# Preparation of the next token block, ordered behind the feed-forward unit it was handed over with

## The chip, the cores and the metric

The kernel runs on one core of a Trainium2 chip. The number that counts is the device time of one execution, in microseconds (us); of several runs the median is given. The engines are called by the profile's names too: TensorE is PE (its weight loads PEld), VectorE is DVE, ScalarE is ACT, GpSimd is POOL, and SyncE, which here only issues DMA transfers, is SP. Each engine runs its instructions strictly in the order of its own queue.

## The reference

One layer of a hybrid decoder: RG-LRU and sliding-window attention side by side, a memory cross-attention, and a gated ConvFFN. It runs for a prompt of 2048 tokens and for 8 samples of 4 tokens (32 more), with a model width of 1024 and a feed-forward width of 3072. The change touches the last part alone:

```python
n3 = rmsnorm(x, p['g_ffn'])
g, ffn_state = causal_dwconv(n3 @ p['w_ffn_gate'], ffn_prev, p['w_ffn_conv'], p['b_ffn_conv'])
x = x + (jax.nn.gelu(g) * (n3 @ p['w_ffn_up'])) @ p['w_ffn_down']
```

The convolution is three taps wide along the tokens. Everything is computed in float32; a product of two matrices is made of three products of rounded parts (a high part and the residual that is left).

## The kernel before, in words

**Phases.** Phase 1 and phase 2 hold the mixers and the cross-attention. Phase 3 is the ConvFFN, from 1078 us of the profiled span to its end. It works on three blocks of tokens (`SB3`: 696, 692 and 660 + 32 columns; blocks 0, 1 and 2 here), and for each block runs a plan of 24 gate units and 12 down units, in the order gate, gate, down. That group of three is called a pair here. A gate unit (`_P3.gate_up`) forms 128 rows of the gate and of the up projection at once by a scheme of seven products of half the width, in place of eight; a down unit (`_P3.down`) multiplies the gated rows of two gate units with their part of the down weights, in eight groups of columns, each of which VectorE adds to `acc` (L1422).

**The gate unit.** TensorE writes the seven products into four areas of the buffers `pg` (one unit's worth in all, so that the next unit waits until they are read). ScalarE copies the first one (`u`, L1372) and half of the gate (`gb`, L1382); VectorE adds the others (`u`, `up`, `gb`, all by `add`, L1353); POOL sets the two columns ahead of the block (L1366, L1368) and keeps the last two (`fcarry`, L1392). Then the convolution and its activation (`gc`: ScalarE L1396, VectorE twice L1398, ScalarE L1399), the product with `up` (L1400), and its split into `ah` (ScalarE) and `al` (VectorE).

**Weights.** Raw weights come by SP into `wr` (L590). For the seven products VectorE forms sums `ws` (L605), and each is split into `pc`, high part by ScalarE (L79), residual by POOL or VectorE (L83). In block 0 the sums' parts are stored for the later blocks (`kept_s`, L616), which load them.

**The preparation.** The seven products need seven operands made from the normalized tokens. `p3_prep(s)` makes them for one block, in four groups of eight steps. A group loads two pieces of the tokens (`x2d`), VectorE scales each by the gain and the norm (`x`, L768), POOL forms differences and sums (`sub`, L756), and `put` splits each of the seven results into `n3s`: ScalarE copies the high part (L79), POOL subtracts for the residual (L83), SP stores it to DRAM (`opd`, L761). That is 8 `x`, 16 `sub`, 28 copies, 28 residuals and 28 stores a block. Pieces `x` and results `n3s` share four buffers. The stored operands are loaded back in the last gate unit of the block (`p3_ops`).

**Where it is handed over.** `p3_prep` is a generator. While block s runs, the preparation of block s + 1 is advanced by one step after the second and one after the fifth product of gate units 4 to 19:

```python
elif 4 <= i < 20 and e % 3 == 1:
    next(ready, None)
```

The preparation of block 0 runs in phase 2 in the same way.

**What sets the order.** The program's order is not the order of the queues. The framework's scheduler goes through time by a model of its own when the kernel is built, and takes for each engine the first instruction in program order that is ready, so one that stands later in the program but is ready sooner goes ahead. A dependency without a semaphore between two instructions of the same engine (`behind`) fixes their order in the queue and nothing else.

## Time and profile before

| | |
|---|---|
| median of 3 runs | 2738.78 us (2737.75 to 2747.58) |
| profiled execution | 2745.93 us |
| its span | 2744.2 us |
| mean granted clock of TensorE | 0.977 |
| busy: TensorE, VectorE, ScalarE, POOL | 95%, 55%, 40%, 35% |
| stores `opd`: number, size, issue to landing | 56, 346 KB, 3.6 us |

The profile comes from one execution, whose own time stands beside its span; its rows are compared with each other, and the medians with medians. A share of busy time is an average over phases. An instruction's row in a timeline gives in brackets how long its engine idled before it and what ended that. L with a number is the line of the kernel that issued an instruction; L137, L79 and L83 are helpers that record the matmul, the high part and the residual for many callers, so there the tile's name tells them apart.

### The profile page before, as it was taken

The page shows a single profiled execution, that of the slowest core. Times are in us where ns is not written, and L with a number is a line of the kernel's source. Part 1 is how long each engine was busy: PE and PEld are TensorE (multiplying, and loading weights), DVE is VectorE, ACT ScalarE, POOL GpSimd, SP SyncE. Part 2 cuts the span into 40 slices and gives each one's busy share as a digit, 9 for nine tenths or more (in the row PEclk, how much of TensorE's full clock was granted, in tenths as well). Part 3 has the DMA queues.
Part 4 walks back from the last instruction along what each step waited for, and adds up shares of the span by engine and source line. Part 5 has one row for each costly group of instructions (what it writes and reads, how often), then busy time and mean ns, then how long its engine had stood idle before and what let it go on. Part 6 is the DMA issues. An engine that isn't in the chain of part 4 may idle for free.

```text
span 2744.2 us, 40972 instructions
## 1 busy us (share of the span) xinstructions
PE 2611.7 (95%) x15221; PEld 2407.4 (88%) x15221; DVE 1518.5 (55%) x2633; ACT 1085.6 (40%) x2071; POOL 954.5 (35%) x928
## 2 busy tenths in 40 slices
PE   7999999998999998888999999999999989999997
PEld 5778888977998887888999998899999989999997
DVE  6476766585442525767676755454444444444445
ACT  5454745474332434443334343333232323232233
POOL 2422211031402344466333344553232424333333
PEclk8899999998999999999999999999999999999998
DMA  6674545366747788766444487764444765444442
GB/s 234 241 230 168 183 158 173 109 243 245 258 165 245 255 268 306 272 242 209 183 161 177 146 314 252 254 216 162 150 160 158 289 214 164 159 158 167 149 154 83
DMA packets 195671, 553.72 MB, mean 202 GB/s; under 512 B 28628, under 2 KB 49364, under 8 KB 192784
## 3 DMA queue, kind: packets, MB, share of 16 engines
q1 hardware_dynamic: 195472, 551.10, 57.9%
q8 instruction: 120, 1.97, 0.3%
q14 instruction: 79, 0.65, 0.1%
HBM read 409.22 MB, written 141.80 MB: 201 GB/s over the span
## 4 chain that ended last, share of the span: by engine, by line
PE 69%; DVE 11%; DMA 6%; issue 4%; ACT 4%; POOL 4%; SPq 1%; POOLq 0%; DVEq 0%; ACTq 0%
PE pg L137 23%; PE pd L137 17%; PE pin L137 10%; PE po L137 5%; PE pmo L137 3%; PE pq L137 3%; DVE gc L1398 3%; POOL pc L83 2%; PE sc L137 1%; DMA x<-x2d 1%; ACT gc L1396 1%; DMA opd<-n3s 1%; POOL x L756 1%; POOL n3s L83 1%; PE tp L853 1%
## 5 line engine op out<-in xcount | busy, mean ns | idle before, releaser
L137 PE MATMUL pg<-n,pc 128*128 128x346 f32 (+1 forms) x6048 | 1022.0, 327 | 48.2 <-DVE up L1353 16.1
L137 PEld LDWEIGHTS pg<-n,pc 128*128 128x128 f32 x6048 | 965.6, 189 | 92.6 <-DVE up L1353 28.2
L83 POOL TENSOR_TENSOR pc<-wr,pc 128x512 fp32r<-128x512 f32 x312 | 411.0, 1322 | 451.4 <-ACT pc L79 446.2
L137 PE MATMUL pd<-ah,pc 128*128 128x346 f32 (+1 forms) x2240 | 467.7, 325 | 18.7 <-DVE acc L1422 12.9
L137 PEld LDWEIGHTS pd<-ah,pc 128*128 128x128 f32 x2240 | 379.4, 191 | 24.7 <-DVE acc L1422 17.6
L79 ACT ACTIVATE pc<-wr 128x512 fp32r<-128x512 f32 x312 | 195.3, 629 | 503.3 <-PE pd L137 236.7
L1422 DVE TENSOR_TENSOR acc<-pd,acc 128x692 f32<-128x692 f32 (+1 forms) x280 | 245.0, 878 | 175.6 <-PE pd L137 172.7
L137 PE MATMUL pd<-al,pc 128*128 128x346 f32 (+1 forms) x1120 | 271.6, 324 | 0.0
L137 PEld LDWEIGHTS pd<-al,pc 128*128 128x128 f32 x1120 | 196.6, 191 | 0.0
L1398 DVE SCALAR_TENSOR_TENSOR gc<-gb,pp,gc 128x696 f32<-128x696 f32 (+2 forms) x144 | 150.1, 1043 | 82.8 <-ACT gc L1396 79.0
L137 PE MATMUL pin<-n1h,wh 128*128 128x512 f32 (+1 forms) x560 | 188.9, 363 | 5.6 <-DVE ql L83 1.8
L137 PE MATMUL pin<-n1h,wl 128*128 128x512 f32 (+1 forms) x560 | 185.8, 358 | 2.8 <-POOL wl L83 2.8
L137 PE MATMUL pin<-n1l,wh 128*128 128x512 f32 (+1 forms) x560 | 186.6, 359 | 1.5 <-DVE n1l L83 1.5
L83 POOL TENSOR_TENSOR wl<-wr,wh 128x1024 fp32r<-128x1024 f32 x35 | 84.7, 2426 | 218.7 <-ACT wh L79 190.8
L1353 DVE TENSOR_TENSOR u<-pg,u 128x346 f32<-128x346 f32 (+1 forms) x144 | 74.3, 516 | 141.0 <-PE pg L137 140.5
L83 POOL TENSOR_TENSOR pc<-ws,pc 128x512 fp32r<-128x512 f32 x72 | 94.5, 1312 | 158.7 <-ACT pc L79 140.6
L1353 DVE TENSOR_TENSOR up<-pg,u 128x346 f32<-128x346 f32 (+1 forms) x144 | 74.1, 515 | 123.5 <-PE pg L137 123.5
L79 ACT ACTIVATE pc<-ws 128x512 fp32r<-128x512 f32 x144 | 90.0, 627 | 113.1 <-PE pg L137 70.0
L137 PEld LDWEIGHTS pin<-n1h,wh 128*128 128x128 f32 x560 | 103.1, 193 | 23.5 <-DVE ql L83 2.4
L1353 DVE TENSOR_TENSOR gb<-pg,u 128x314 f32<-128x314 f32 (+2 forms) x96 | 38.9, 426 | 145.5 <-PE pg L137 145.5
L137 PEld LDWEIGHTS pin<-n1h,wl 128*128 128x128 f32 x560 | 102.6, 193 | 18.8 <-POOL wl L83 3.8
L137 PEld LDWEIGHTS pin<-n1l,wh 128*128 128x128 f32 x560 | 102.7, 194 | 17.1 <-DVE n1l L83 2.6
(317 smaller groups left out, 4196.0 us busy)
## 6 DMA issues: line engine op xcount, KB each, us to landing
pc<-kept_s SPq DMA_DIRECT2D x192, 512.0 KB, 4.3
kept_s<-pc SPq DMA_DIRECT2D x96, 512.0 KB, 3.0
wh<-keeph SPq DMA_DIRECT2D x90, 512.0 KB, 4.0
wl<-keepl SPq DMA_DIRECT2D x90, 512.0 KB, 5.0
wr<-in_w_gate_dram SPq DMA_DIRECT2D x72, 512.0 KB, 3.8
wr<-in_w_down_dram SPq DMA_DIRECT2D x72, 512.0 KB, 4.0
opd<-n3s SPq DMA_DIRECT2D x56, 346.0 KB, 3.6
n<-opd SPq DMA_DIRECT2D x14, 1384.0 KB, 11.2
```

Source lines behind the costliest of these rows:

```text
L79: nc.scalar.activation(hi, src, AF.Copy)
L83: return e.tensor_tensor(out=lo, in0=src, in1=hi.bitcast(F), op=OP.subtract).ins
L137: nc.tensor.matmul(o, w[a], xs, start=first and n == 0, stop=last and n == 2, skip_group_check=more)
L756: sub = lambda o, x, y, op=OP.subtract: nc.gpsimd.tensor_tensor(out=o, in0=x, in1=y, op=op)
L853: nc.tensor.transpose(tp[:, j], st[:, j, c * 128:(c + 1) * 128], K.ident)
L1353: add = lambda o, p, t: nc.vector.tensor_tensor(out=o, in0=p, in1=t, op=OP.add)
L1396: nc.scalar.activation(gc, gb[:, 2:2 + NW], AF.Identity, scale=K.col(C_FW, 48 + f), bias=K.col(C_FB, f))
L1398: nc.vector.scalar_tensor_tensor(gc, gb[:, k:k + NW], K.col(C_FW, 24 * k + f), gc, op0=OP.mult, op1=OP.add)
L1422: nc.vector.tensor_tensor(out=v, in0=pd[:, :, 0:H], in1=v, op=OP.add)
```

## The change

Each of the preparation's operations on VectorE, ScalarE and POOL is given an order dependency on the latest marked operation of its own engine in the gate unit that is being written when the step is handed over. The marks are, on VectorE, each addition `add`; on ScalarE, the copies `u` and `gb`; on POOL, the two columns ahead of the block and the carry. `put` has its two operations written out in place of the helper `split`, so that each can be given its dependency. Loads and stores get none. In phase 2 no marks are set, so the preparation of block 0 gets none either. In the changed kernel the lines of phase 3 stand some lines lower: the scaling is L774, the copies `n3s` are L765, the residuals L766, the stores L767, `add` L1362, `gc` L1408, `acc` L1432.

```diff
--- before.py
+++ after.py
@@ -508,6 +508,7 @@
             self.nc.sync.dma_start(self.x1s, self.I["x"][:, :, SEQ:T].rearrange("k p t -> p k t"))
             smp = _MemSample(self)
             self.xpool = lambda: dict(pool=self.wraw, tag="wr")
+            self.mark = {}
             ready = self.p3_prep(0)
 
             def prep(n=1):
@@ -753,11 +754,16 @@
             a = self.xpool()
             return a.pop("pool").tile(shape, dtype, name=name, **a)
 
-        sub = lambda o, x, y, op=OP.subtract: nc.gpsimd.tensor_tensor(out=o, in0=x, in1=y, op=op)
+        def after(eng, ins):
+            self.behind(ins, self.mark.get(eng), "preparation order")
+
+        def sub(o, x, y, op=OP.subtract):
+            after("pool", nc.gpsimd.tensor_tensor(out=o, in0=x, in1=y, op=op))
 
         def put(nm, k, src):
             t = tile_([128, 2, H], R, "n3s")
-            self.split(src, t[:, 0], t[:, 1], "act", "pool")
+            after("act", nc.scalar.activation(t[:, 0], src, AF.Copy))
+            after("pool", nc.gpsimd.tensor_tensor(out=t[:, 1], in0=src, in1=t[:, 0].bitcast(F), op=OP.subtract))
             nc.sync.dma_start(self.opd[s][BUDDY.index(nm)][:, 2 * k:2 * k + 2], t.bitcast(F))
 
         for k in range(KT // 2):
@@ -765,7 +771,7 @@
             for kk in (k, k + KT // 2):
                 x = tile_([128, W], F, "x3")
                 self.p3_dma(x, [d[kk] for d in self.x2d], t0, W)
-                nc.vector.scalar_tensor_tensor(x, x, self.col(G_FFN, kk), rt, op0=OP.mult, op1=OP.mult)
+                after("dve", nc.vector.scalar_tensor_tensor(x, x, self.col(G_FFN, kk), rt, op0=OP.mult, op1=OP.mult))
                 xs += [x[:, 0:H], x[:, H:W]]
             b11, b12, b21, b22 = xs
             yield
@@ -1350,7 +1356,11 @@
         xy = K.psum([128, 2, 512], "pg", "pg")
         zw = K.psum([128, 2, 512], "pg", "pg")
         X, Y, Z, V = (t[:, e, 0:H] for t in (xy, zw) for e in range(2))
-        add = lambda o, p, t: nc.vector.tensor_tensor(out=o, in0=p, in1=t, op=OP.add)
+        mark = K.mark
+
+        def add(o, p, t):
+            mark["dve"] = nc.vector.tensor_tensor(out=o, in0=p, in1=t, op=OP.add).ins
+
         tmp = lambda nm: q2.tile([128, H], F, name=nm, tag="hv", bufs=3)
 
         def product(i, out, first):
@@ -1363,13 +1373,13 @@
 
         gb = q2.tile([128, NW + 2], F, name="gb")
         if s == 0:
-            nc.gpsimd.memset(gb[:, 0:2], 0.0)
+            mark["pool"] = nc.gpsimd.memset(gb[:, 0:2], 0.0).ins
         else:
-            nc.gpsimd.tensor_copy(gb[:, 0:2], K.p3c[s - 1][:, f])
+            mark["pool"] = nc.gpsimd.tensor_copy(gb[:, 0:2], K.p3c[s - 1][:, f]).ins
         up = q1.tile([128, W], F, name="up")
         product(0, X, True)
         u = tmp("u")
-        nc.scalar.activation(u, X, AF.Copy)
+        mark["act"] = nc.scalar.activation(u, X, AF.Copy).ins
         product(1, Y, True)
         u2 = tmp("u2")
         add(u2, Y, u)
@@ -1379,7 +1389,7 @@
         product(3, V, True)
         add(up[:, H:W], V, u4)
         product(4, X, False)
-        nc.scalar.activation(gb[:, 2:2 + H], X, AF.Copy)
+        mark["act"] = nc.scalar.activation(gb[:, 2:2 + H], X, AF.Copy).ins
         product(5, Z, False)
         n = w - H
         add(gb[:, 2 + H:2 + w], Z[:, 0:n], u2[:, 0:n])
@@ -1389,7 +1399,7 @@
             bt = lambda t: t[:, n:H].rearrange("p (b t) -> p b t", t=NT)
             add(gv[:, :, 2:6], bt(Z), bt(u2))
             nc.gpsimd.tensor_copy(K.sfo[:, f], gv[:, :, 4:6])
-        nc.gpsimd.tensor_copy(self.carry[:, f], gb[:, w:w + 2])
+        mark["pool"] = nc.gpsimd.tensor_copy(self.carry[:, f], gb[:, w:w + 2]).ins
         product(6, V, False)
         add(up[:, 0:H], V, u2)
         gc = q1.tile([128, NW], F, name="gc")
```

The order of the queues, as built, at three places in block 0. The names with numbers are buffers: `x_12431` and `x_12435` are the two pieces of the second group, `t_12497` is its difference, `opd_1` and so on are the stored operands.

ScalarE, around the copies of the second group, in the kernel before:

```order
L79 ACTIVATE n3s<-x_12431 128x346
L79 ACTIVATE pc<-wr 128x512
L79 ACTIVATE pc<-ws 128x512
L79 ACTIVATE n3s<-x_12431 128x346
L1372 ACTIVATE u<-pg 128x348
L79 ACTIVATE pc<-wr 128x512
L79 ACTIVATE n3s<-t_12497 128x346
L79 ACTIVATE pc<-wr 128x512
L79 ACTIVATE pc<-ws 128x512 x2
L79 ACTIVATE n3s<-x_12431 128x346
L1382 ACTIVATE gb<-pg 128x348
```

and in the changed one:

```order
L1382 ACTIVATE u<-pg 128x348
L765 ACTIVATE n3s<-x_12431 128x346
L79 ACTIVATE pc<-wr 128x512
L765 ACTIVATE n3s<-t_12497 128x346
L79 ACTIVATE pc<-wr 128x512
L79 ACTIVATE pc<-ws 128x512 x2
L1392 ACTIVATE gb<-pg 128x348
L79 ACTIVATE pc<-ws 128x512
L79 ACTIVATE pc<-wr 128x512
```

Before, four copies `n3s` stand among eleven rows, two of them ahead of `u`; after, two stand behind `u`, and none in the rest of that unit.

VectorE, where the second group is scaled, before:

```order
L1422 TENSOR_TENSOR acc<-pd,acc 128x696
L605 TENSOR_TENSOR ws<-wr 128x512
L768 SCALAR_TENSOR_TENSOR x_12431<-x_12431,pp,rt 128x692
L1422 TENSOR_TENSOR acc<-pd,acc 128x696
L605 TENSOR_TENSOR ws<-ws,wr 128x512
L1422 TENSOR_TENSOR acc<-pd,acc 128x696
L768 SCALAR_TENSOR_TENSOR x_12435<-x_12435,pp,rt 128x692
L1422 TENSOR_TENSOR acc<-pd,acc 128x696
```

and after:

```order
L1408 SCALAR_TENSOR_TENSOR gc<-gb,pp,gc 128x696 x2
L1362 TENSOR_TENSOR up<-pg,u_12275 128x348
L83 TENSOR_TENSOR pc<-ws,pc 128x512
L1410 TENSOR_TENSOR up<-up,gc 128x696
L774 SCALAR_TENSOR_TENSOR x_12431<-x_12431,pp,rt 128x692
L774 SCALAR_TENSOR_TENSOR x_12435<-x_12435,pp,rt 128x692
L83 TENSOR_TENSOR al<-up,ah 128x696
L1362 TENSOR_TENSOR u_12439<-pg,u 128x348
L1362 TENSOR_TENSOR u_12456<-pg,u_12439 128x348
```

The two scalings stood between the additions `acc` of a down unit; now they stand side by side in a gate unit, behind its product `up<-up,gc` and ahead of `al`.

SP, its stores `opd` and loads around the second group's stores before:

```order
L590 DMA wr<-in_w_gate_dram 128x1024
L761 DMA opd_6_11526<-n3s 128x692
L616 DMA kept_s_3_12417<-pc 128x1024
L590 DMA wr<-in_w_up_dram 128x1024
L731 DMA x_14233<-x2d_68 128x328
L731 DMA x_14233<-x2d_69 128x364
L731 DMA x_14237<-x2d_68 128x328
L731 DMA x_14237<-x2d_69 128x364
L590 DMA wr<-in_w_gate_dram 128x1024
L590 DMA wr<-in_w_up_dram 128x1024
```

and after:

```order
L617 DMA kept_s_0_12776<-pc 128x1024
L767 DMA opd_2_11522<-n3s 128x692
L617 DMA kept_s_1_12798<-pc 128x1024
L617 DMA kept_s_2_12819<-pc 128x1024
L591 DMA wr<-in_w_gate_dram 128x1024
L617 DMA kept_s_3_12871<-pc 128x1024
L767 DMA opd_3_11523<-n3s 128x692
L591 DMA wr<-in_w_up_dram 128x1024
L767 DMA opd_4_11524<-n3s 128x692
```

Before, the second group's last store (`opd_6`) is followed by the loads of the fourth group's pieces (`x_14233`, `x_14237`) within a few rows; after, one or two stores of the second group stand between the raw weights' loads, and no pieces are loaded there.

## Rows read from the trace of the kernel before

**Rows 1.** The page of the whole span: busy time, share of the span and instructions of each engine, and the shares of the chain that ended last.

```profile
PE 2611.7 (95%) x15221; PEld 2407.4 (88%) x15221; DVE 1518.5 (55%) x2633; ACT 1085.6 (40%) x2071; POOL 954.5 (35%) x928
...
PE 69%; DVE 11%; DMA 6%; issue 4%; ACT 4%; POOL 4%; SPq 1%; POOLq 0%; DVEq 0%; ACTq 0%
```

**Rows 2.** Busy time by stretch in block 0 of the feed-forward phase. The first three stretches are one pair each (two gate units and a down unit), the last is the five pairs behind them. Columns: start and end, us; length, us; then for PE, PEld, DVE, ACT and POOL busy us (instructions); granted clock of PE; DMA share; GB/s.

```profile
1150.23:1202.50 52.27, 46.52 (x270) 44.07 (x269) 40.14 (x49) 21.82 (x38) 32.92 (x31) 0.97 0.64 232
1202.50:1256.06 53.56, 45.17 (x272) 42.60 (x271) 38.50 (x43) 21.83 (x39) 34.85 (x33) 1.00 0.64 224
1256.06:1310.74 54.68, 46.46 (x261) 44.13 (x261) 36.18 (x42) 21.05 (x38) 33.94 (x32) 0.94 0.64 220
1310.74:1531.94 221.20, 218.37 (x1323) 209.63 (x1322) 147.79 (x200) 88.39 (x140) 81.64 (x81) 1.00 0.46 167
```

**Rows 3.** The same view and columns in block 1: three pairs, and two pairs in one stretch.

```profile
1715.79:1765.09 49.30, 44.80 (x265) 43.49 (x265) 22.74 (x28) 17.43 (x31) 28.65 (x31) 0.97 0.77 255
1765.09:1811.61 46.52, 43.70 (x266) 41.91 (x265) 24.63 (x30) 17.16 (x32) 30.13 (x32) 1.00 0.72 242
1811.61:1855.64 44.03, 43.04 (x266) 42.01 (x265) 19.62 (x26) 14.05 (x24) 16.97 (x18) 1.00 0.55 188
1855.64:1942.50 86.86, 86.17 (x531) 84.12 (x530) 39.08 (x52) 25.55 (x40) 27.08 (x29) 1.00 0.49 158
```

**Rows 4.** What TensorE waited for in the three pairs of block 0 (1150.23 to 1310.74 us). Columns: engine, operation and line, what it waited for: us in total, times, longest us.

```profile
PE pd L137 <- DVE acc L1422: 7.0, 5, 2.5
PE pg L137 <- DVE gb L1353: 5.8, 5, 1.8
PE pg L137 <- DVE up L1353: 3.6, 4, 2.4
PE pg L137 <- ACT u L1372: 3.3, 1, 3.3
PE pg L137 <- DVE u L1353: 2.5, 2, 1.5
```

**Rows 5.** The first line of the same view for block 1's three pairs (1715.79 to 1855.64 us).

```profile
PE pd L137 <- DVE acc L1422: 5.6, 3, 3.5
```

**Rows 6.** Groups by line on ScalarE in the three pairs of block 0, shapes apart: the copies `n3s`. Columns: line, engine, operation, out<-in with shapes, count | busy us, mean ns of one | idle us just before them and what ended it.

```profile
L79 ACT ACTIVATE n3s<-x 128x346 fp32r<-128x346 f32 x24 | 11.8, 490 | 30.8 <-POOL x L756 12.3 <-DMA opd<-n3s 10.8 <-DVE x L768 7.7
...
L79 ACT ACTIVATE n3s<-t 128x346 fp32r<-128x346 f32 x4 | 1.9, 483 | 0.0
```

**Rows 7.** The same view on POOL: the preparation's residuals, subtractions and additions.

```profile
L83 POOL TENSOR_TENSOR n3s<-x,n3s 128x346 fp32r<-128x346 f32 x24 | 26.4, 1108 | 9.5 <-ACT n3s L79 9.5
...
L756 POOL TENSOR_TENSOR x<-x,x 128x346 f32<-128x346 f32 x8 | 8.5, 1068 | 6.8 <-DVE x L768 4.9 <-issue 1.5
L83 POOL TENSOR_TENSOR n3s<-t,n3s 128x346 fp32r<-128x346 f32 x4 | 5.2, 1300 | 0.0
L756 POOL TENSOR_TENSOR t<-x 128x346 f32<-128x346 f32 x4 | 4.3, 1067 | 5.8 <-DVE x L768 5.8
L756 POOL TENSOR_TENSOR x<-x 128x346 f32<-128x346 f32 x4 | 4.0, 1010 | 0.3
```

**Rows 8.** The same view on VectorE: an operation of the gate, `gc`, and the preparation's scaling `x`.

```profile
L1398 DVE SCALAR_TENSOR_TENSOR gc<-gb,pp,gc 128x696 f32<-128x696 f32 x12 | 15.2, 1265 | 7.4 <-ACT gc L1396 7.3
...
L768 DVE SCALAR_TENSOR_TENSOR x<-x,pp,rt 128x692 f32<-128x692 f32 x8 | 8.4, 1056 | 0.6 <-DMA x<-x2d 0.6
```

**Rows 9.** Timeline around TensorE's stop before 1207.84 us, block 0, rows of four engines in order of time. Columns: start us, length us, engine, line, operation, out<-in, count [idle before <-what ended it].

```profile
1202.30 0.94 DVE L768 SCALAR_TENSOR_TENSOR x<-x,pp,rt 128x692 f32<-128x692 f32 x1 [0.61 <-DMA x<-x2d]
...
1204.36 1.36 POOL L756 TENSOR_TENSOR x<-x,x 128x346 f32<-128x346 f32 x1
...
1206.95 0.49 ACT L79 ACTIVATE n3s<-x 128x346 fp32r<-128x346 f32 x1 [3.62 <-POOL x L756]
...
1207.84 4.47 PE L137 MATMUL pg<-n,pc 128*128 128x348 f32 x26 [3.27 <-ACT u L1372]
```

**Rows 10.** Timeline around TensorE's stop before 1751.97 us, block 1, same columns: ScalarE, VectorE twice, TensorE.

```profile
1745.42 0.49 ACT L79 ACTIVATE n3s<-x 128x346 fp32r<-128x346 f32 x1 [3.55 <-POOL x L756]
...
1747.71 1.91 DVE L1398 SCALAR_TENSOR_TENSOR gc<-gb,pp,gc 128x692 f32<-128x692 f32 x1 [4.51 <-ACT gc L1396]
...
1751.06 0.87 DVE L1422 TENSOR_TENSOR acc<-pd,acc 128x692 f32<-128x692 f32 x1
...
1751.97 0.82 PE L137 MATMUL pd<-ah,pc 128*128 128x346 f32 x2 [3.53 <-DVE acc L1422]
```

**Rows 11.** Groups by line on VectorE in three pairs of block 0 without preparation (1354.88 to 1487.70 us): `gc`.

```profile
L1398 DVE SCALAR_TENSOR_TENSOR gc<-gb,pp,gc 128x696 f32<-128x696 f32 x12 | 12.6, 1051 | 6.8 <-ACT gc L1396 6.6
```

**Rows 12.** Timeline of VectorE in one of those pairs: the product's low part `al`, a weight sum `ws`, and the gate's end with the first `acc` of the down unit.

```profile
1417.04 1.12 DVE L83 TENSOR_TENSOR al<-up,ah 128x696 fp32r<-128x696 f32 x1 [0.85 <-ACT ah L79]
...
1420.63 1.06 DVE L605 TENSOR_TENSOR ws<-wr 128x512 f32<-128x512 f32 x1 [1.01 <-DMA wr<-in_w_up_dram]
...
1426.75 2.15 DVE L1398 SCALAR_TENSOR_TENSOR gc<-gb,pp,gc 128x696 f32<-128x696 f32 x2 [1.10 <-ACT gc L1396]
...
1430.64 1.67 DVE L1422 TENSOR_TENSOR acc<-pd,acc 128x696 f32<-128x696 f32 x2
```

**Rows 13.** What SP's queue waited for in the three pairs of block 0: the line of the stores `opd`. Columns as in rows 4.

```profile
SPq L761 <- POOL n3s L83: 21.6, 12, 4.3
```

**Rows 14.** The same line for block 1's three pairs.

```profile
SPq L761 <- POOL n3s L83: 35.9, 16, 5.8
```

## The prediction

> **What bounds the kernel now.** I read the busy shares of the whole page first [rows 1]. TensorE is busy for 95% of the span, and the chain that ended last runs through it for 69%; VectorE follows with 11%. So time can only be won where TensorE stands still or runs slow, and the question is what it waits for in the stretch that the change touches.
>
> That stretch is the feed-forward phase, and there I read busy time pair by pair, a pair being two gate units and the down unit that follows. In block 0, three pairs in a row take 52.27, 53.56 and 54.68 us and the next five take 221.20 us together, 44.24 each [rows 2]. The work of TensorE is the same in all eight. What differs is the other engines: POOL is busy 33 to 35 us in each of the three and 16.3 in each of the five, VectorE 36 to 40 against 29.6, ScalarE 21 to 22 against 17.7. Block 1 shows the same twice, in smaller: 49.30, 46.52 and 44.03 us, then 86.86 for two pairs, 43.43 each [rows 3].
>
> The groups by line say whose work it is. All eight of VectorE's scalings `x`, all 28 copies `n3s` of ScalarE and all 44 preparation operations of POOL for block 1 lie in those three pairs [rows 6 to 8]. The program hands this work over in units 4 to 19, which is eight pairs, and the queue packs it into the first three.
>
> The excess is my budget. Block 0: 160.51 - 3 x 44.24 = 27.8 us. Block 1: 139.85 - 3 x 43.43 = 9.6 us. Together **37.4 us**. It divides by TensorE's own columns. In block 0 its busy time is 138.15 against 3 x 43.67 = 131.0, so 7.1 us are longer matmuls, where the granted clock is 0.97 and 0.94, and 20.7 us are standing still. The list of its waits agrees: 22.2 us in the three pairs, 7.0 of them for `acc`, 11.9 for VectorE's additions `gb`, `up` and `u`, and 3.3 in one piece for ScalarE's `u` [rows 4]. In block 1 the largest entry is again `acc`, 5.6 us in three waits [rows 5].
>
> How such a wait comes about is plain in two chains. At 1207.84 TensorE had stood for 3.27 us for `u` on ScalarE; `u` had been ready to run, but a copy `n3s` stood ahead of it in ScalarE's queue and waited 3.62 us for POOL's `x`, and that for VectorE's scaling at 1202.30, which itself waited 0.61 us for its load [rows 9]. In block 1 an `n3s` held ScalarE for 3.55 us until 1745.42; the activation `gc` of the gate came behind it, VectorE's `gc` sat idle 4.51 us for that, `acc` came behind `gc`, and TensorE stood 3.53 us for `acc` [rows 10]. Head-of-line blocking by preparation work, in an order that the build chose.
>
> **The change part by part.** It adds no operation and removes none: 8 scalings, 28 copies, 28 residuals, 16 subtractions and additions and 28 stores per block remain. The added dependencies are order on one engine, so they cost no instruction. What moves: each preparation operation now stands behind the gate unit in which it is handed over. The listed order shows one or two copies `n3s` per unit on ScalarE, close behind `u`, where they stood between almost all operations; the two scalings of a group stand side by side on VectorE between the product `up<-up,gc` and `al`, once in two pairs; and the queue of SP carries a store `opd` or two per unit in place of bursts.
>
> What goes: the three dense pairs of block 0 and the two to three of block 1. If the spread pairs cost nothing, all 37.4 us go. That is the bound on one side.
>
> What is late next, in block 0. Each of its eight pairs now gets an eighth of the work. ScalarE: 28 x 490 ns / 8 = 1.7 us on 17.7 of 44.2; it has room, and a copy behind `u` finds its source finished a unit earlier, as the scaling stands in the unit before. POOL: 44 operations of 1.0 to 1.3 us [rows 7], 48.4 us / 8 = 6.1 us on 16.3; room too. VectorE: one scaling of 0.94 us per pair, as it ran at 1202.30 [rows 9], on 29.6. What is not hidden by itself is the slower VectorE beside a busy POOL. `gc` took 1265 ns in the dense pairs and 1051 in the others [rows 8, 11]. Over all: VectorE's busy time in the three pairs is 114.8 us; less 3 x 29.6 and 8 x 0.94 for the scalings, 18.6 us are stretch, for 44 POOL operations. If that much recurs, it is 2.3 us per pair. Not all of it delays TensorE. In a pair without preparation, the run from `gc` at 1426.75 to the end of `acc` at 1432.3 is the one on which TensorE's restart hangs [rows 12]: 5.6 of VectorE's 29.6 us, so 0.19 x 2.3 = 0.44 us per pair. The two scalings take 1.88 us ahead of `al`, before which VectorE idles 0.85 us [rows 12]: 1.0 us late, in every second pair, 0.5 per pair if all of it arrives. So between 0 and 0.94 us by this working; I take 0.75, nearer the upper end, because the stretches that wait for weights are tight too: 8 x 0.75 = **6 us**. The hard bounds are 0 and the whole stretch of 18.6 us; the bound beyond (that spreading saves nothing) is a rival.
>
> Block 1: its VectorE is busy 19.5 us of 43.4, and its stretch in the three pairs was 66.99 - 3 x 19.54 - 6 x 0.94 = 2.7 us; six scalings, as the three pairs have 84 VectorE instructions and three quiet ones 78 [rows 3]. Its third pair gives a second measure: POOL worked 16.97 - 13.54 = 3.4 us on preparation there and the pair lost 0.6 us [rows 3]; in proportion, 6.1 us per pair would lose 1.1, and eight pairs 8.6. I take **3 us** of bounds 0 and 8.6, nearer the stretch, as that pair also ends what the dense ones left behind.
>
> The stores. A store `opd` waits in SP's queue for POOL's residual, 21.6 us in 12 waits with a longest of 4.3 in block 0, and 35.9 in 16 with a longest of 5.8 in block 1 [rows 13, 14]. In the new order a store stands ahead of a weight load in each pair. I cost this at nothing: the residual is the next of POOL's operations behind a finished copy, and the loads are issued some units ahead; if the cover is gone, the price is the slower rival's. The copies' own wait for a free buffer (10.8 us of their idle time ended with a store's landing [rows 6]) goes, as the four buffers `x` now turn over twice per unit and not as fast as the queue allows.
>
> Sum: 37.4 - 6 - 3 = 28.4 us. The profiled execution took 2745.93 us (span 2744.2, and 1.7 outside it): 2745.9 - 28.4 = 2717.5. The median of the runs is 2738.78, 7.15 below that execution, and by the same gain **2710 us**. A part of the budget is slow clock, 7.1 us in block 0 and 2.3 in block 1 (131.54 us busy against 3 x 43.09); how much of that the median run had is not shown, and the range allows for its absence.
>
> **One rule weighed.** The rows show VectorE's instructions longer while POOL works (`gc` 1265 against 1051 ns [rows 8, 11]). The Trainium skill, "SBUF — State Buffer", section "Who interferes with whom", says that a VectorE instruction with two SBUF inputs contends with a GpSimd instruction that reads SBUF, that whoever issues first keeps the shared pair for its whole instruction, and that the other blocks. By that, the sum of the stretch would depend on how many operations meet and not on how dense they are; `gc` reads two such inputs, and here the trace agrees. By the rule the sum would keep the whole stretch, which is rival (a); by the rows of the edge it keeps a third.
>
> **The rivals.**
> (a) The stretch is kept whole. POOL's 44 operations meet VectorE's as often when spread, and every delay reaches TensorE: 18.6 + 2.7 us stay, the gain is 37.4 - 21.3 = 16 us, 2723. For it: VectorE is the engine that most of the waits name [rows 4]. Against it: VectorE idles 14.7 us of each quiet pair, and not all of its work is awaited.
> (b) The price is per step, not per density. Each of 64 steps costs 37.4 / 64 = 0.58 us wherever it stands, and nothing changes: 2739. For it: each chain of rows 9 and 10 starts with one ordinary step. Against it: block 1's third pair, with 3.4 us of POOL's preparation, lost 0.6 us, and its first, with 15.1, lost 5.9 [rows 3]: 0.18 and 0.39 us for each.
> (c) All is hidden: 2738.8 - 37.4 = 2701. For it: every engine but TensorE has room in each pair. Against it: block 0's VectorE, idle 14.7 us a pair, has less room than block 1's, idle 23.9, and even there the third pair lost something.
> (d) **Slower**, by SP's queue. A store that waits for POOL now stands ahead of a weight load in each of 16 pairs. VectorE in a quiet pair already waits 1.0 us for a weight load [rows 12], so a load held up is passed on. If each pair loses the longest wait of block 0, 4.3 us, it is 69 us against 37.4 won: 2770. It decides from 37.4 / 16 = 2.3 us a pair; the means of the waits are 21.6 / 12 = 1.8 and 35.9 / 16 = 2.2 [rows 13, 14]. Against it: those waits arose while four buffers were turned over as fast as possible.
> That the change does not do what it says is excluded by the order itself.
>
> **How the numbers follow.** The forecast, 2710 with an own range of 2702 to 2719: 0.55. (c) 0.12, (a) 0.13, (b) 0.12, (d) 0.08. A difference of 0.5%, 13.7 us, is about what a measurement of this kernel can tell from no change, so faster means under 2725.1: forecast, (a) and (c), 0.80. Same: (b), 0.12. Slower: (d), 0.08. For 8 in 10 the range takes in the forecast, (a) and (c) with some room: 2698 to 2728.
>
> **What would show it.** In the profile after, all eight pairs of block 0 with preparation take about 45 us and those of block 1 about 43.6; POOL's busy time is about 22 us in each, and not 33 and 16. ScalarE's idle time ahead of `n3s` for POOL's `x` is gone, and so is TensorE's wait of 3.3 us for `u`. TensorE's waits for `acc` shrink to a few tenths each. `gc` lies between 1051 and 1265 ns. If the pairs stand at 46 us and more, (a) or (b) holds: with `gc` still near 1265 ns it is the stretch, otherwise the steps. If SP's waits for `n3s` are long and VectorE's `ws` waits for `wr` by 2 us and more, it is (d). The prediction is wrong if the eight pairs of block 0 do not come out alike.

## The result, and the profile after

The changed kernel takes 2725.4 us (median of 6 runs, 2716.98 to 2729.83) where the kernel before, run beside it, takes 2744.6 (2737.75 to 2747.58): a ratio of 0.9925, with a 95% interval of 0.9906 to 0.9945 (the quotient of the two medians is 0.9930). It is faster by 19.2 us, or 0.7%. The forecast was 28.4 us of gain and 2710; the time lies inside the range of 2698 to 2728, near its upper end, and outside the forecast's own range of 2702 to 2719.

The profiled execution took 2723.25 us, its span 2721.5. Against the 2744.2 of before that is 22.7 us less, but not all of it lies where the change does. The first gate product starts at 1078.2 us in the profile of before and at 1068.9 here, though up to there every queue has the same order in both kernels. From that start to the end of the span, **1666.0 us became 1652.6, 13.4 less**: 11.7 in block 0 (571.4 to 559.8), 0.9 in block 1 (539.4 to 538.5), 0.9 in block 2. The control e8 below settles what the other 9.3 us are.

The busy shares and the chain, the two lines that answer to [rows 1]:

```profile
PE 2601.2 (96%) x15221; PEld 2399.2 (88%) x15221; DVE 1532.7 (56%) x2633; ACT 1084.4 (40%) x2071; POOL 969.6 (36%) x928
...
PE 72%; DVE 11%; ACT 5%; issue 5%; DMA 4%; POOL 2%; SPq 1%; POOLq 0%; DVEq 0%; ACTq 0%
```

TensorE works 10 us less, at a mean granted clock of 0.981 in place of 0.977, and holds 72% of the chain in place of 69%. VectorE, which has the same instructions as before, is busy 14 us longer.

Busy time by stretch, five of the pairs of block 0 with their preparation, which answer to [rows 2] (columns as there):

```profile
1141.08:1190.52 49.44, 45.63 (x273) 43.17 (x273) 38.82 (x47) 18.97 (x31) 25.37 (x21) 1.00 0.51 188
1190.52:1235.11 44.59, 43.33 (x265) 41.55 (x263) 32.96 (x40) 19.17 (x32) 22.59 (x21) 1.00 0.54 198
1235.11:1283.08 47.97, 45.58 (x268) 43.86 (x267) 32.74 (x42) 18.95 (x31) 24.32 (x22) 0.96 0.54 191
...
1327.68:1374.50 46.82, 44.10 (x267) 42.26 (x267) 34.68 (x42) 18.94 (x31) 25.09 (x22) 1.00 0.55 196
1374.50:1419.10 44.60, 43.30 (x265) 41.55 (x264) 32.94 (x40) 19.17 (x32) 22.60 (x21) 1.00 0.53 197
```

The dense pairs of 52 to 55 us are gone, and POOL is busy 22 to 25 us everywhere. But the pairs are not alike: 49.4, 44.6, 48.0, 44.6, 46.8, 44.6, 46.8, 45.2. Every second one is long, and the third has a granted clock of 0.96 besides. Block 1 shows the same in smaller, against [rows 3]:

```profile
1696.81:1741.41 44.60, 43.16 (x265) 41.94 (x265) 22.58 (x28) 13.16 (x21) 18.51 (x18) 1.00 0.48 162
1741.41:1785.32 43.91, 43.26 (x267) 42.05 (x265) 19.96 (x26) 14.20 (x24) 18.40 (x19) 1.00 0.56 189
1785.32:1829.91 44.59, 43.15 (x265) 41.95 (x265) 22.72 (x28) 13.91 (x23) 20.12 (x20) 1.00 0.59 194
```

The long pairs have 28 instructions of VectorE in block 1 and 42 in block 0 (47 in the first), the others 26 and 40: the two scalings of a group. What TensorE waits for in the eight pairs of block 0, which answers to [rows 4]:

```profile
PE pg L137 <- DVE u L1362: 7.4, 10, 2.0
PE pd L137 <- DVE acc L1432: 4.3, 6, 1.2
PE pg L137 <- DVE up L1362: 4.2, 10, 1.0
```

The 3.3 us for ScalarE's `u` do not occur any more, and `acc` fell from 7.0 us in three pairs to 4.3 in eight. At the top stands a wait for VectorE's sums `u`, 7.4 us. In block 1 the entry `acc` of [rows 5] is gone altogether, and `u` leads there too:

```profile
PE pg L137 <- DVE u L1362: 7.4, 10, 1.6
PE pg L137 <- DVE up L1362: 3.1, 9, 0.3
```

ScalarE's copies `n3s`, which had 30.8 us of idle time ahead of them in [rows 6], have 0.3 (groups by line, same columns):

```profile
L765 ACT ACTIVATE n3s<-x 128x346 fp32r<-128x346 f32 x22 | 10.7, 486 | 0.3
...
L765 ACT ACTIVATE n3s<-t 128x346 fp32r<-128x346 f32 x4 | 1.9, 481 | 0.0
```

So the blocking at the head of ScalarE's queue, the mechanism of [rows 9, 10], is removed completely. What replaces it is on VectorE. Its groups in the same eight pairs, against [rows 8, 11]:

```profile
L1408 DVE SCALAR_TENSOR_TENSOR gc<-gb,pp,gc 128x696 f32<-128x696 f32 x32 | 37.8, 1181 | 18.2 <-ACT gc L1406 17.6
...
L83 DVE TENSOR_TENSOR al<-up,ah 128x696 fp32r<-128x696 f32 x16 | 19.8, 1237 | 3.8 <-ACT ah L79 3.8
...
L774 DVE SCALAR_TENSOR_TENSOR x<-x,pp,rt 128x692 f32<-128x692 f32 x8 | 10.6, 1361 | 1.4 <-DMA x<-x2d 1.4
```

`gc` takes 1181 ns (1265 dense, 1051 alone), and a scaling takes 1361 ns in the mean, more than the 1056 of the dense order. That mean hides two lengths: the first scaling of each long pair takes 0.93 us, the second 1.97 to 1.98 in three of them and 1.23 in the third, where it waited 1.4 us for its load. One long pair of block 0 shows the path, VectorE first and then TensorE (timeline, columns as in rows 9):

```profile
1344.44 2.83 DVE L774 SCALAR_TENSOR_TENSOR x<-x,pp,rt 128x692 f32<-128x692 f32 x2
1347.19 1.48 DVE L83 TENSOR_TENSOR al<-up,ah 128x696 fp32r<-128x696 f32 x1
1348.58 1.13 DVE L1362 TENSOR_TENSOR u<-pg,u 128x348 f32<-128x348 f32 x2
...
1356.90 3.32 DVE L1408 SCALAR_TENSOR_TENSOR gc<-gb,pp,gc 128x696 f32<-128x696 f32 x2 [1.10 <-ACT gc L1406]
...
1361.96 1.66 DVE L1432 TENSOR_TENSOR acc<-pd,acc 128x696 f32<-128x696 f32 x2
```

```profile
1349.14 6.09 PE L137 MATMUL pg<-n,pc 128*128 128x348 f32 x36 [1.15 <-DVE u L1362]
...
1362.89 0.59 PE L137 MATMUL pd<-ah,pc 128*128 128x348 f32 x2 [1.16 <-DVE acc L1432]
```

The two scalings take 2.83 us, `al` behind them 1.48, and only then come the sums `u`; TensorE has stood 1.15 us for the first of them when it goes on at 1349.14. Later in the same pair the two `gc` take 3.32 us in place of 2.15 [rows 12], `acc` is late, and TensorE stands another 1.16.

The four long pairs share the first of these two stops and not the second. The longest wait for `u` is 1.16, 1.98, 1.15 and 1.11 us in the first, third, fifth and seventh pair. A stop of 1.1 us for `acc` stands in the fifth and the seventh alone; the first has one of 1.01 for `up` instead. In the third pair, 0.6 us behind the stop of 1.98, the granted clock was at the lower of its two levels, 1.2 GHz, for 3.4 us, and TensorE is busy 45.58 us in that pair where the fifth has 44.10. The stretch at the lower level (columns as in rows 2):

```profile
1258.02:1261.43 3.41, 3.41 (x14) 3.40 (x13) 2.50 (x2) 0.00 (x0) 3.41 (x3) 0.50 0.07 27
```

SP's stores `opd` wait for POOL's residual as in [rows 13, 14], in the eight pairs of block 0 and in block 1:

```profile
SPq L767 <- POOL n3s L766: 24.1, 22, 2.5
```

```profile
SPq L767 <- POOL n3s L766: 63.5, 26, 6.2
```

### The profile page after: what moved, and what is told of

Same layout as the page of the kernel before. It is cut to its first block, busy times and chain, and to the rows that moved or that the text cites. A ratio compares the mean times of both kernels' runs of the same rounds, so it can differ in the third digit from the quotient of the medians.

```text
span 2721.5 us, 41002 instructions
## 1 busy us (share of the span) xinstructions
PE 2601.2 (96%) x15221; PEld 2399.2 (88%) x15221; DVE 1532.7 (56%) x2633; ACT 1084.4 (40%) x2071; POOL 969.6 (36%) x928
## 3 DMA queue, kind: packets, MB, share of 16 engines
q8 instruction: 120, 1.97, 0.3%
## 4 chain that ended last, share of the span: by engine, by line
PE 72%; DVE 11%; ACT 5%; issue 5%; DMA 4%; POOL 2%; SPq 1%; POOLq 0%; DVEq 0%; ACTq 0%
PE pg L137 24%; PE pd L137 19%; PE pin L137 10%; PE po L137 6%; PE pmo L137 3%; DVE gc L1408 3%; PE pq L137 3%; PE sc L137 1%; ACT gc L1406 1%; POOL pc L83 1%; DVE al L83 1%; DMA x<-x2d 1%; PE tp L859 1%; ACT pc L79 1%; DMA x<-in_x_dram 1%
## 5 line engine op out<-in xcount | busy, mean ns | idle before, releaser
L83 POOL TENSOR_TENSOR pc<-wr,pc 128x512 fp32r<-128x512 f32 x312 | 419.2, 1352 | 425.7 <-ACT pc L79 424.8
L1432 DVE TENSOR_TENSOR acc<-pd,acc 128x692 f32<-128x692 f32 (+1 forms) x280 | 244.9, 877 | 178.2 <-PE pd L137 176.5
L1408 DVE SCALAR_TENSOR_TENSOR gc<-gb,pp,gc 128x696 f32<-128x696 f32 (+2 forms) x144 | 150.6, 1046 | 78.5 <-ACT gc L1406 76.1
L1362 DVE TENSOR_TENSOR u<-pg,u 128x346 f32<-128x346 f32 (+1 forms) x144 | 74.2, 515 | 130.7 <-PE pg L137 128.9
L1362 DVE TENSOR_TENSOR up<-pg,u 128x346 f32<-128x346 f32 (+1 forms) x144 | 74.1, 514 | 124.0 <-PE pg L137 124.0
L1362 DVE TENSOR_TENSOR gb<-pg,u 128x314 f32<-128x314 f32 (+2 forms) x96 | 38.8, 425 | 150.9 <-PE pg L137 150.9
```

Source lines behind the costliest of these rows:

```text
L83: return e.tensor_tensor(out=lo, in0=src, in1=hi.bitcast(F), op=OP.subtract).ins
L1362: mark["dve"] = nc.vector.tensor_tensor(out=o, in0=p, in1=t, op=OP.add).ins
L1408: nc.vector.scalar_tensor_tensor(gc, gb[:, k:k + NW], K.col(C_FW, 24 * k + f), gc, op0=OP.mult, op1=OP.add)
L1432: nc.vector.tensor_tensor(out=v, in0=pd[:, :, 0:H], in1=v, op=OP.add)
```

## The experiments

Four lengths from each profile are compared, besides the time: *nine pairs* of block 0, from the end of the first pair's predecessor (1150.23 in the profile of before, 1141.08 after) over the eight pairs with preparation and one more; *ten pairs* of block 1, from the end of block 0's last down unit; the *last nine* of these; and *phase 3*, from the first gate product to the end of the span. All times are in us. A ratio is that to the kernel before, with its interval.

| kernel | nine pairs | ten pairs | last nine | phase 3 | time, ratio |
|---|---|---|---|---|---|
| before | 425.7 | 466.4 | 400.2 | 1666.0 | |
| e8, before again | 428.7 | 467.3 | 401.1 | 1670.0 | 2741.04 (one run) |
| changed | 413.9 | 465.5 | 397.4 | 1652.6 | 2725.4, 0.9925 (0.9906 to 0.9945) |
| e1, no preparation | 399.1 | 457.9 | 390.5 | 1628.9 | 2706.84, 0.9857 (0.9838 to 0.9875) |
| e2, no scalings | 412.2 | 459.6 | 393.8 | 1646.7 | 2720.95, 0.9906 (0.9889 to 0.9922) |
| e3, half a unit later | 414.4 | 461.9 | 396.0 | 1649.7 | 2728.21, 0.9930 (0.9914 to 0.9946) |
| e4, ScalarE alone | 415.3 | 464.5 | 397.4 | 1652.0 | 2726.4, 0.9925 (0.9910 to 0.9941) |
| e5, no POOL | 409.1 | 461.4 | 394.3 | 1643.6 | 2722.64, 0.9914 (0.9896 to 0.9932) |
| e6, no stores | 416.5 | 464.8 | 397.8 | 1653.5 | 2732.38, 0.9947 (0.9927 to 0.9968) |
| e7, residuals on VectorE | 413.9 | 459.5 | 393.7 | 1648.9 | 2722.21, 0.9915 (0.9899 to 0.9932) |
| e9, scalings apart | 409.9 | 463.3 | 396.2 | 1646.5 | 2722.69, 0.9921 (0.9903 to 0.9939) |
| e10, one unit later | 405.5 | 462.0 | 394.9 | 1642.4 | 2719.3, 0.9905 (0.9879 to 0.9931) |
| e11, down units only | 415.0 | 459.0 | 391.9 | 1645.9 | 2724.18, 0.9928 (0.9909 to 0.9946) |
| e12, e10 and residuals | 406.7 | 459.0 | 392.1 | 1639.2 | 2714.72, 0.9896 (0.9878 to 0.9914) |

Each length comes from one profile. The kernel before, which has two, differs by 3.0, 0.9, 0.9 and 4.0 us between them, so two rows that differ by less tell little by their lengths alone. The first of the ten pairs is not to be read for the preparation at all: in the changed kernel it holds none, and its length goes by the clock, 65.8 to 66.2 us in the profiles where its granted clock is 1.00, 66.9 to 67.4 at 0.97, and 68.1 at 0.95, which is the changed kernel's. Its row there and in e2 (columns as in rows 2):

```profile
1628.67:1696.81 68.14, 63.27 (x375) 60.79 (x374) 34.66 (x47) 22.00 (x35) 23.15 (x22) 0.95 0.76 249
```

```profile
1635.60:1701.46 65.86, 60.95 (x375) 58.15 (x374) 35.12 (x47) 22.00 (x35) 24.00 (x23) 1.00 0.78 257
```

**e8, the control.** The kernel before, unchanged.

> The kernel before, unchanged, profiled once more. The feed-forward phase started at 1078.2 us in its first profile and at 1068.9 in the changed kernel's, though all queues stand in the same order up to there. If that difference is the spread of single executions, this one starts anywhere from 1068 to 1079, and from there to the end of the span takes 1666 us within 2. If it belongs to the kernel before, it starts at 1077 to 1079 again.

Phase 3 started at 1069.3 us and took 1670.0. So the start is a spread of single executions: over the fourteen profiles of this study it lies between 1068.9 and 1079.6, without relation to what was edited. The 9.3 us are not the change's, and what the change does in phase 3 is 13.4 or 17.4 us by the one or the other profile of before. The length of 1670 is 4 over the 1666 that was expected to come back within 2. Most of that lies in the second of the dense pairs, which took 52.3, 56.0 and 55.4 this time. TensorE's stops in the second come to 8.4 us in the first profile and to 8.2 in this one; what differs is its granted clock, 0.94 in place of 1.00 (against the second of rows 2):

```profile
1194.98:1251.01 56.03, 47.76 (x271) 45.20 (x270) 39.44 (x43) 21.81 (x39) 33.66 (x33) 0.94 0.60 214
```

The medians' difference of 19.2 us, with an interval of some 15 to 26, holds 17.4 and not 13.4; why the stretch ahead of phase 3 varies was not tried.

**e1, the budget.** The preparation of blocks 1 and 2 is left out:

```diff
-                        ready = self.p3_prep(s + 1) if s < 2 else iter(())
+                        ready = iter(())
+                        if s < 2:
+                            self.opd[s + 1] = [t[:, :, 0:346] for t in self.opd[0]]
```

> The preparation of blocks 1 and 2 is left out (their operands are loaded from block 0's), so this shows what the feed-forward phase costs without it. Blocks 0 and 1 took 571.4 and 539.4 us in the kernel before and 559.8 and 538.5 in the changed one (from the first gate product of a block to that of the next). If the pairs without preparation are the right base, as the budget of 37.4 us assumed, block 0 falls to 543 to 545 us and block 1 to 529 to 531, and the time to about 37 us under the kernel before. If something else in these pairs is slow (their place early in a block), block 0 stays above 550.

Phase 3 is 1666.0 - 1628.9 = 37.1 us shorter than before (41.1 against e8); the budget was 37.4. Of the 37.1, 26.6 lie in the nine pairs of block 0 and 9.7 in the last nine of block 1. Blocks 0 and 1 take 544.9 and 530.8 us, as was written. The first pair and all nine:

```profile
1146.31:1192.47 46.16, 44.78 (x270) 42.60 (x269) 34.94 (x45) 18.48 (x30) 19.16 (x17) 1.00 0.52 194
...
1146.31:1545.36 399.05, 393.80 (x2381) 377.75 (x2381) 272.21 (x365) 159.97 (x254) 149.86 (x145) 1.00 0.47 171
```

The first pair takes 46.16 us even so and has 45 instructions of VectorE, 34.9 us: it is slower by itself. And it gives the price that the changed kernel still pays: 14.8 us in nine pairs, 7.7 in the ten of block 1 and 6.9 in their last nine, 23.7 in the phase. By pairs of block 0: 3.3, 0.6, 3.9, 0.6, 2.7, 0.6, 2.6, 0.9.

**e2, no scalings.** In `p3_prep`, for blocks 1 and 2 the scaling is left out:

```diff
-                after("dve", nc.vector.scalar_tensor_tensor(x, x, ...))
+                if s == 0:
+                    after("dve", nc.vector.scalar_tensor_tensor(x, x, ...))
```

> The changed kernel with the 8 scalings per block on VectorE left out for blocks 1 and 2 (their operands come from unscaled tokens). Theory 1, the two scalings side by side ahead of al and u are what remains of the cost: the four slow pairs of block 0 (46.8 to 49.4 us) fall to 44.6 like the four between them, block 0 to 547 to 549 us (559.8 now), block 1 to 533 to 536 (538.5). Theory 2, VectorE's operations are stretched by POOL's 44 operations wherever they stand: the slow pairs stay at 46 or more, block 0 at 556 or more.

Block 1 fell to 532.6 us, near theory 1's 533 to 536, though 2.3 us of that are the clock of its first pair: of the 6.9 us in the last nine, 3.6 are gone. Block 0 did not come out as theory 1 said: 412.2, with the first pair at 49.9 (its mean granted clock is 0.97) and the others at 45.1 to 45.9. Behind the first, the long pairs lost 1.2 us or more, and the short ones between them gained 0.5 or more. Without the scalings POOL's preparation starts sooner in the long pairs, and its residuals of the weights come in a row behind it, beside `ws` and up to `gc`:

```profile
1264.77 0.94 POOL L761 TENSOR_TENSOR x<-x,x 128x346 f32<-128x346 f32 x1
1265.78 0.80 POOL L761 TENSOR_TENSOR x<-x 128x346 f32<-128x346 f32 x1
1266.53 6.37 POOL L83 TENSOR_TENSOR pc<-wr,pc 128x512 fp32r<-128x512 f32 x4
```

```profile
1273.29 2.70 DVE L1409 SCALAR_TENSOR_TENSOR gc<-gb,pp,gc 128x696 f32<-128x696 f32 x2 [1.10 <-ACT gc L1407]
```

Those two `gc` take 2.70 us. So in block 0 neither theory holds alone.

**e5, no POOL.** For blocks 1 and 2, POOL's subtractions, additions and residuals are left out, and the store sends the high part twice (where the difference `t` would be copied, another piece is):

```diff
         def sub(o, x, y, op=OP.subtract):
-            after("pool", nc.gpsimd.tensor_tensor(out=o, in0=x, in1=y, op=op))
+            if s == 0:
+                after("pool", nc.gpsimd.tensor_tensor(out=o, in0=x, in1=y, op=op))
...
-            after("pool", nc.gpsimd.tensor_tensor(out=t[:, 1], ...))
+            if s == 0:
+                after("pool", nc.gpsimd.tensor_tensor(out=t[:, 1], ...))
```

> The changed kernel with POOL's 16 subtractions and additions and 28 residuals left out for blocks 1 and 2 (the stores send the high part twice); loads, scalings, copies and stores stay. Nine pairs of block 0 take 425.7 us in the kernel before, 413.9 in the changed one, 412.2 without the scalings and 399.1 without any preparation. Theory A, POOL's operations are what is left in block 0 (they slow VectorE beside them and hold up POOL's residuals of the weights, and so the weight loads): the nine pairs fall to 401 to 405. Theory B, the price is that of loads and stores on SP's queue ahead of the weight loads: they stay at 410 or more. Theory C, the scalings and POOL's operations cost as much each: 406 to 410.

Theory C: 409.1. Behind the first (48.4), the long pairs stand at 46.0, the others at 44.5 to 45.0. VectorE and TensorE in a long pair (timelines):

```profile
1261.98 2.82 DVE L779 SCALAR_TENSOR_TENSOR x<-x,pp,rt 128x692 f32<-128x692 f32 x2
1264.73 1.96 DVE L83 TENSOR_TENSOR al<-up,ah 128x696 fp32r<-128x696 f32 x1
...
1274.84 2.15 DVE L1413 SCALAR_TENSOR_TENSOR gc<-gb,pp,gc 128x696 f32<-128x696 f32 x2 [1.10 <-ACT gc L1411]
```

```profile
1267.18 6.00 PE L137 MATMUL pg<-n,pc 128*128 128x348 f32 x36 [1.59 <-DVE u L1367]
```

This takes the path apart. Without POOL's preparation `gc` is back at 2.15 us for two and the stop for `acc` is gone; but the scalings take 2.82 us as before, `al` even 1.96, and TensorE stands 1.59 us for `u`. So the stop for `u` comes with the scalings, and the stop for `acc`, in the two pairs that have it, with POOL's preparation.

**e6, no stores.** The 28 stores of blocks 1 and 2 are left out:

```diff
-            nc.sync.dma_start(self.opd[s][BUDDY.index(nm)][...], t.bitcast(F))
+            if s == 0:
+                nc.sync.dma_start(self.opd[s][BUDDY.index(nm)][...], t.bitcast(F))
```

> The changed kernel with the 28 stores opd per block left out for blocks 1 and 2 (their operands are loaded from block 0's); everything else of the preparation stays. Theory B (SP's queue and the transfers): the nine pairs of block 0 fall from 413.9 us to 405 or less. Theory A (POOL's operations): they stay within 2 us of 413.9.

416.5, no fall but 2.6 us more, just outside both theories (the queues were built anew, and those of TensorE and VectorE came out in a slightly different order). The stores cost nothing that shows; as the order moved too, a price of a few us is not excluded.

**e4, which engine's order counts.** Only ScalarE's operations are held back:

```diff
         def after(eng, ins):
-            self.behind(ins, self.mark.get(eng), "preparation order")
+            if eng == "act":
+                self.behind(ins, self.mark.get(eng), "preparation order")
```

> The order is held on ScalarE alone; VectorE's and POOL's preparation is left to the scheduler. If ScalarE's queue carries the gain (its copies hold the four shared buffers and so pace the rest), block 0 is within 3 us of the changed kernel's 559.8 us. If each engine's own order is needed, block 0 is 565 or more, near the 571.4 of the kernel before.

Block 0 takes 560.5 us from its first product (559.8 changed, 571.4 before), phase 3 as long as in the changed kernel, and the pairs alternate as there, 45.2, 46.8, 44.6 and 47.1 behind the first. ScalarE's order alone carries the gain. That it does so because its copies hold the shared buffers, and so pace the scalings and POOL, is the reason written ahead; it was not tried by itself.

**e3, half a unit later.** The steps are handed over after the fifth product and the second product of the next unit:

```diff
-                        elif 4 <= i < 20 and e % 3 == 1:
+                        elif e == 4 and 4 <= i < 20 or e == 1 and 5 <= i < 21:
```

> The changed kernel with every step handed over half a unit later (after the fifth product of units 4 to 19 and the second of units 5 to 20), which puts the scalings behind the addition up of the middle of a unit, where VectorE idles, and not ahead of al and u. Nothing is left out. Theory 1 (place of the scalings): the slow pairs fall to 45 us or less, block 0 to 547 to 552 us, the time by 8 to 12 us under the changed kernel. Theory 2 (POOL's stretch, wherever they stand): block 0 stays within 3 us of 559.8. A third way: the scalings delay gb and with it gc, and pairs grow to 48.

Block 1 won 1.4 us in its last nine pairs, block 0 nothing: its long pairs are 47.5 us behind the first, near the 48 of the third way. There the scalings stand ahead of `gb` now, beside the weight sums, and TensorE waits 5.8 us for `gb`, up to 1.4 at once. Moving work from one awaited operation to another did not help; that led to the next three, which ask for the place and not the amount.

**e9, the scalings apart.**

```diff
+        def scale(x, kk):
+            after("dve", nc.vector.scalar_tensor_tensor(x, x, ...))
...
-                after("dve", nc.vector.scalar_tensor_tensor(x, x, ...))
+                if kk == k:
+                    scale(x, kk)
...
+            scale(x, kk)
             sub(b12, b22, b12)
```

> The changed kernel with the second scaling of each group handed over two steps later, with the third step, so that one scaling of 0.94 us stands ahead of al and the other between the additions acc of the following down unit. Nothing is left out. Theory P (place: what stands ahead of al, u, gc and acc is paid one to one, as these have no slack, and the rest is free): VectorE idles 0.85 us ahead of al, so a single scaling costs about 0.1 us there; the slow pairs fall from 46.8 to 45.3 us or less, the nine pairs of block 0 from 413.9 to 405 to 409, the ten of block 1 from 465.5 to 460 to 462. Theory Q (amount: so much work of VectorE and POOL per pair costs so much wherever it stands): nine pairs 412 to 416.

409.9 and 463.3, each about 1 us above theory P's figures and, in block 0, below Q's. The pairs come out between 44.9 and 45.9 behind the first; the alternation is gone. In the fifth pair, a single scaling ahead of `al` (VectorE, then POOL):

```profile
1345.80 0.94 DVE L770 SCALAR_TENSOR_TENSOR x<-x,pp,rt 128x692 f32<-128x692 f32 x1
1346.74 1.90 DVE L83 TENSOR_TENSOR al<-up,ah 128x696 fp32r<-128x696 f32 x1
...
1345.83 2.07 POOL L83 TENSOR_TENSOR pc<-wr,pc 128x512 fp32r<-128x512 f32 x1 [1.52 <-ACT pc L79]
```

POOL's residual starts 0.03 us behind the scaling and is busy along all of it, and yet the scaling takes 0.94 us; `al`, which follows while the residual is still going on, takes 1.90. In the changed kernel it is the second scaling that stands in that place.

**e10, one unit later.**

```diff
-                        elif 4 <= i < 20 and e % 3 == 1:
+                        elif 5 <= i < 21 and e % 3 == 1:
```

> The changed kernel with every step handed over one gate unit later (units 5 to 20 in place of 4 to 19), one number changed. The order shows both scalings of a group between the additions acc of a down unit, behind al, and POOL's first subtractions with them, where POOL idles 6.4 us twice. Theory P: the slow pairs fall to 45.2 us or less, nine pairs of block 0 to 403 to 408 (one more pair carries work at the end), block 1 to 459 to 462, the time to 8 to 13 us under the changed kernel. Theory Q: nine pairs 412 to 416. A third way: a scaling between two acc delays the second, and TensorE waits for acc by some 0.9 us twice per group: 411 to 415, with the waits under acc.

405.5, as theory P said, with the same operations and one number changed; block 1 at 462.0, the end of its range, and the time 6.1 us below the changed kernel's where 8 to 13 were expected (the intervals of the two ratios overlap). A scaling in its new place (timeline of VectorE), and what TensorE waits for in seven of the pairs:

```profile
1276.77 0.88 DVE L83 TENSOR_TENSOR al<-up,ah 128x696 fp32r<-128x696 f32 x1
1277.56 0.94 DVE L774 SCALAR_TENSOR_TENSOR x<-x,pp,rt 128x692 f32<-128x692 f32 x1
1278.41 0.88 DVE L1432 TENSOR_TENSOR acc<-pd,acc 128x696 f32<-128x696 f32 x1
1279.20 0.94 DVE L774 SCALAR_TENSOR_TENSOR x<-x,pp,rt 128x692 f32<-128x692 f32 x1
```

```profile
PE pg L137 <- DVE up L1362: 2.6, 7, 0.4
PE pg L137 <- DVE u L1362: 2.6, 7, 0.4
PE pd L137 <- DVE acc L1432: 1.5, 7, 0.2
```

The scalings take 0.94 us each, between `acc` and `acc`, where POOL does little; TensorE's seven waits for `acc` come to 1.5 us, and no wait is longer than 0.4. All pairs behind the first take 44.6 to 45.2.

**e11, all of it in the down units.**

```diff
-                        elif 4 <= i < 20 and e % 3 == 1:
-                            next(ready, None)
+                        elif 5 <= i < 20 and i % 2 and e == 0:
+                            for _ in range(4):
+                                next(ready, None)
```

> The changed kernel with four steps handed over at once, ahead of the first sum of every odd unit from 5 to 19, so that all of the preparation may run in the down units. Theory P: nine pairs of block 0 at 401 to 405 us, the lowest of all with the whole preparation, as gc is no longer stretched beside POOL's operations in the gate unit (its mean falls from 1181 to under 1100 ns). Against it: four steps need four buffers n3s and two are free, so a copy waits for a store's landing (3.6 us) at the head of ScalarE's queue; if that falls on the next unit's u, the pairs stand at 46 us and more and ScalarE's idle time ahead of n3s names opd.

Block 0 went wrong, 415.0, though its `gc` was shorter (1128 ns, not the 1100 hoped for). The groups of ScalarE and TensorE's waits say why:

```profile
L766 ACT ACTIVATE n3s<-x 128x346 fp32r<-128x346 f32 x24 | 11.4, 491 | 39.0 <-POOL x L762 23.6 <-DVE x L775 9.8 <-DMA opd<-n3s 5.6
```

```profile
PE pd L137 <- DVE acc L1433: 14.0, 12, 2.1
```

A copy waits at the head of ScalarE's queue again, 39.0 us in all, mostly for POOL's `x` and less for a store's landing than was written; TensorE pays at `acc`, 14.0 us. Block 1 gains, 459.0.

**e7 and e12, the residuals.** In e7 those of both blocks go to VectorE; e12 is e10 with those of block 2's preparation alone:

```diff
-            after("pool", nc.gpsimd.tensor_tensor(out=t[:, 1], ...))
+            if s < 2:
+                after("pool", nc.gpsimd.tensor_tensor(out=t[:, 1], ...))
+            else:
+                after("dve", nc.vector.tensor_tensor(out=t[:, 1], ...))
```

> The changed kernel with the 28 residuals n3s of blocks 1 and 2 on VectorE and not on POOL. Nothing is left out. POOL then keeps 16 of its 44 operations. Theory A: the nine pairs of block 0 fall to 405 to 409 us if VectorE's added 3.5 operations of half a microsecond per pair find room in its 14.7 us of idle time, and block 1 to 461 to 464 us (465.5 now; ten pairs with the one that spans the change of block). Theory B: 413 to 416 us. A third way: VectorE is the engine awaited, so more work there costs more than POOL's: 418 us or more.

> The kernel of e10 (one unit later) with the 28 residuals of block 2's preparation, which run in block 1, on VectorE and not on POOL; block 0 as in e10. Nothing is left out. Theory P: VectorE idles 23.9 us of a pair in block 1, and a residual of half a microsecond finds room behind al; ten pairs of block 1 fall from 462.0 us in e10 to 459 to 460.5, as with the same edit alone (459.5 in e7); nine pairs of block 0 stay at 405 to 406; the time is 2 to 3 us under e10's, and at or below any other with the whole work. Theory Q: block 1 stays at 461.5 or more.

In e7 block 0 stayed at 413.9. That is theory B's figure, but e6 had left nothing of theory B; that POOL's relief and VectorE's burden cancel is the reading that remains, and was not tried by itself. Block 1 fell to 459.5, below what was expected, 3.7 us of it in the last nine pairs. e12 keeps both gains, 459.0 and 406.7 (0.7 us over what was expected and 1.2 over e10, in two of its pairs), and has the lowest median with the whole work: 2714.72 us, a ratio of 0.9896, where the change alone has 0.9925. The intervals of these two still touch (0.9914 and 0.9906).

## Why the prediction was right, and where it was not

**The number had room.** The time lies in the range because the range was made to take in rivals (a) and (c); the forecast's own 2702 to 2719 was missed. Of the 15 us between forecast and time, 5.8 are the base, a median of 2738.78 where the runs beside the changed kernel have 2744.6; the other 9.2 are gain that did not come. And by the sign that the prediction set for itself, that the eight pairs of block 0 come out alike, it was wrong. What was right is the mechanism of the gain.

**The budget stands.** The excess of the dense pairs is the price of the preparation as it was packed: 37.4 us by the rows, 37.1 in e1 (41.1 by the second profile of before).

**What goes, went.** The head-of-line wait of the copies fell from 30.8 us to 0.3, the stop for ScalarE's `u` is gone, and e4 shows that ScalarE's order alone does it.

**The term that was mis-sized is the 6 us for block 0 and the 3 for block 1.** Against e1 they measure 14.8 and, in the last nine pairs of block 1, 6.9: 21.7 in place of 9, so 28.4 - 12.7 = 15.7 us of gain were left, and the phase shows 13.4 to 17.4. Within it, the short pairs cost 0.6 to 0.9 us, close to the 0.75 that was taken. The error is the long pairs, and the sentence that priced them says that the two scalings come 1.0 us late ahead of `al`, "in every second pair, 0.5 per pair if all of it arrives". Three things were wrong in it. The scalings do not take 1.88 us there but 2.8, the second of them 1.98, with POOL's residual of a weight going on beside them (2.82 even without POOL's preparation, in e5; 0.94 each in e10, where POOL does little). `al` behind them is stretched as well, 1.48 us for 1.12. And the run from `gc` to `acc` is not the only one on which TensorE hangs: the sums `u` stand behind `al`, and in [rows 12] only the idle time ahead of `al` was read, not who waits behind it. Each long pair paid 2.6 to 3.9 us; in the third, which paid most, 1.5 of it is longer matmuls at the lower clock. The scalings are not the whole error in block 0, though: two of the long pairs stop 1.1 us for `acc` too, behind a `gc` beside POOL, and without the scalings 13.2 of the 14.8 us stay, spread more evenly (e2). That the pairs would come out alike fell with it; the text named this as what would make it wrong.

**Block 1.** Of its two measures, the smaller was trusted (2.7 of stretch) and the larger, 8.6 in proportion to the third pair, was nearer the truth: 6.9 in the last nine pairs.

**The stretch was sized wrongly too**, and by a base that did not fit. It was taken as 18.6 us against three quiet pairs of 29.6, but the first pair has 34.9 us of VectorE without any preparation (e1). Over nine pairs, VectorE's busy time less e1's 272.2 and 7.5 for the scalings is 292.2 - 279.7 = 12.5 us before, 302.8 - 279.7 = 23.1 in the changed kernel, and 12.8 in e10. Spreading did not keep the stretch, it nearly doubled it; e10, which moves the scalings and POOL's first operations into the down units, has no more than the dense order. That bears on rival (a). The stretch is not fixed by the amount of work, nor does all of it reach TensorE: e10 has as much as the kernel before and costs 6.4 us in nine pairs in place of 26.6. The Trainium skill, "SBUF — State Buffer", section "Who interferes with whom", makes such contention a matter of which instructions meet. These three sums agree with that.

**The rivals.** (a) named the nearest time, 2723, by a mechanism that is half of the truth: the stop for `u` comes with the scalings, the one for `acc` with POOL. They do not add: without the scalings block 0 still pays 13.2 us, without POOL 10.0, with both 14.8. (b), a price per step wherever it stands, falls by e10: the same steps elsewhere cost 6.4. (c) fell by 23.7 us. (d) did not come: the stores' waits were as long as feared in block 1, 63.5 us in 26 waits, and yet no wait for a load is among TensorE's waits there, and e6 won nothing.

## What to carry to other kernels

When background work blocks a queue, pinning it behind the foreground operation it was handed over with removes the blocking, and holding one engine's queue alone did as much here (e4). Where it is pinned matters as much as that it is spread: look up, for each operation that will stand *behind* it, who waits for that one, and put the work where neither that engine's consumers nor its neighbour on the other side (here POOL beside VectorE) is busy. Price the moved operation at what it takes beside its new neighbours, not at its fastest, and take a quiet stretch as base only if it has the same instructions.
